# Two more seven-product steps in the first unit, one more in each of two branch units, and x's rows in two tiles

## The chip, the core and the metric

The kernel runs on one core of a Trainium2 chip. Its engines are named as the profile names them: PE (TensorE, matmuls), PEld (its weight loads), DVE (VectorE), ACT (ScalarE), POOL (GpSimd) and SP (SyncE, which here only issues transfers). The metric is the device time of one execution in microseconds (us).

## The reference

The reference is one hybrid decoder block on x of 256 tokens by 4096 channels, all in float32:

```
h    = rmsnorm(x) * norm_w
proj = h @ w_in                      # 4096 x 20480
u_p, z_p, u_c, b_c, c_c, z_c, g = split(proj)
y_pool = (pool(u_p) @ pool_w, by group) * pool_scale * silu(z_p)
y_conv = b_c * conv3(c_c * u_c) * silu(z_c)
br     = [y_pool @ w_branch[0], y_conv @ w_branch[1]]
merged = sum(sigmoid(g + gate_b) * br)
out    = rmsnorm(x + merged @ w_out) * final_norm_w
```

Nearly all of the work is three products with 256 rows on the left: by w_in, by the two w_branch and by w_out.

## The kernel before

**Units and steps.** The work is a list of units, each 1024 output columns wide: 20 of w_in (`cz0`, `cb0`, `cu0`, `cc0`, `cz1`, ... , the gates `g0_0` to `g1_0`), 8 of w_branch (`b0_0`, `b1_0`, `b0_1`, ... , `b1_3`) and 4 of w_out. A unit is a run of steps; each takes 256 input channels, and with them a 2 by 2 arrangement of weight blocks of 128 by 512. There are 16 steps in a unit of w_in or w_out and 8 in one of w_branch. A string of letters per unit says what kind each step is.

**Products in parts.** A float32 weight block is split in two: ACT writes the rounded "high" part to a cell of `ring` (the `highs` and `rounded` calls) and DVE writes the rest, the "low" part (`low`, `lows`: the profile's TENSOR_TENSOR ring<-raw,ring). The left operand was split in the same way earlier. One product is then three matmuls of 512 columns: high by high, high by low, low by high.

**P and S.** A plain step, P, has 4 blocks by 2 token halves, so 8 products or 24 matmuls, into four PSUM banks (`sums`). A step S does the same with seven products (Strassen's way, in Winograd's form), so 21 matmuls, into those banks and four more (`shared`). For an S step the weights have to be added up: POOL issues a transfer that adds one block to another as it lands (`gather` in `issue_corner`), DVE forms three sums in `parts`, ACT writes their high parts and DVE their low parts. At a unit's end ACT copies the four `shared` banks to tile `J` (`copy_corners`), DVE makes three sums there (`corner_sums`) and adds them to the unit's result (`combine`); a unit of P steps alone has none of that.

**The first unit.** `cz0` runs while x itself is still arriving. Its steps follow `FIRST`: operands 0 to 7 are kept as P operands, 8 to 15 as S operands, and in this unit all 16 are used as P. For an operand of the second kind ACT scales four blocks of x into `sa`, and DVE forms four sums there and writes high and low parts to `arena` (`x_fill`). Operands 14 and 15 have room for eight entries each; 8 to 13 have seven, and the eighth, needed by a P step, goes to a tile `extra`. Beside this, x's rows come in four quarters of 1 MB each into tile `E` (`fetch_rows`), and ACT and DVE square half of each (`square`) for the norm. `root` then gives `rin`, the factor of each token, and ACT scales by it as it empties the four banks into `Y` (`evacuate`; Y<-sums in the profile).

**The branch units.** The left operands of `b0_*` and `b1_*` come back from DRAM in pieces through small staging tiles (`sa`, `sb`, `sc`), as `Fill` objects that are advanced a little after every six matmuls (`pop_fill`). `b1_1` to `b1_3` run "PSPSPSPP", three S steps each. A P operand can also serve as S if its four sums lie in a tile `side`, as in the units of w_in with ten S steps.

**What sets the order.** Every instruction is pinned to the order in which the program makes it, on each engine. `pump` prepares weights up to four steps ahead, as far as the 26 cells of `ring` are free; `tick` pops one entry of a unit's epilogue queue after six matmuls. POOL's and SP's transfers leave in that order too, each behind whatever its engine waits for.

Of the kernel before, what the change touches and what calls it, by code (L numbers as in the profile page):

```python
# [15 lines left out]
P = 128  # L16
# [17 lines left out]
TAIL = 3  # L34

FIRST = (0, 1, 8, 2, 9, 3, 10, 11, 4, 12, 13, 5, 14, 6, 15, 7)
OPENED = 12
EIGHT3 = "PPPSPSSPSPSPSPSS"
NINE = "PSPSPSPSSPSPSSPS"
# [7 lines left out]
B0 = "PPPPSPSP"  # L47
B1 = "PSPSPSPP"
B1_FIRST = "PPSPSPSP"
B0_FOUR = "PPPSSPSS"  # L50


@with_exitstack
def hybrid_block(ctx: ExitStack, tc: tile.TileContext, x, xc, prm, rows_in, w_in, pool_w, w_branch, w_out, out):
# [17 lines left out]
    def sub(dst, a, b):  # L72
        return tt(dst, a, b, ALU.subtract)
# [10 lines left out]
    def move(dst, src):  # L84
        return pin(nc.scalar.dma_start(dst, src))
# [75 lines left out]
    def open_last(dt):  # L161
        stack = ExitStack()
        ctx.enter_context(stack)
        pool = stack.enter_context(tc.tile_pool(name="last", bufs=1, side="right"))
        last_pair.update(stack=stack, tile=pool.tile([P, 8 * KB], dt, name="last_pair"))
# [360 lines left out]
    def gap(n):  # L526
        return [None] * n
# [15 lines left out]
    def sequence(text, np_, total, both):  # L543
        text = [c for c in text if c in "PS"]
        ns = text.count("S")
        assert len(text) == total
        ss = list(range(np_, np_ + ns))
        ps = list(range(np_)) + list(range(np_ + ns, total))
        assert total - np_ - ns <= both
        return [(c, (ss if c == "S" else ps).pop(0)) for c in text]  # L550

    def seq_x(text):
        if text is FIRST:
            return [("P", i) for i in FIRST]
        if text is TEN_B:
            ss = list(range(ND, 13)) + [ND - 1] + list(range(13, 16)) + [ND - 2]
            ps = list(range(ND - 2))
            return [(c, (ss if c == "S" else ps).pop(0)) for c in "".join(text)]
        text = [c for c in text if c in "PS"]
        ns = text.count("S")  # L560
        if ns > NS + NB:
            ss = list(range(ND, 16)) + [resident[0]]
            if ns > NS + NB + 1:
                resident[0] = 2 * ND - 3 - resident[0]
                ss = [ss[-1]] + ss[:-1] + [resident[0]]
            ps = [i for i in range(ND) if i not in ss]
            return [(c, (ss if c == "S" else ps).pop(0)) for c in text]
        return sequence(text, ND, ND + NS + NB, NB)

    def seq_y(text):  # L570
        return sequence(text, 8 - text.count("S"), 8, 0)

    def in_unit(name, col, epi, text, **kw):
# [206 lines left out]
    def branch_unit(n, c):  # L780
        def epi(u):
            if n == 0:
                if c:
                    return gap(4) + [lambda: move(spare(), gates_d[1, c])] + gap(8) + [lambda: mul(Y, E, Y)]
                return gap(12) + [lambda: mul(Y, E, Y)]
            turned = spare() if c < 3 else Y

            def gated():
                mul(E, E, spare())
                if c == 3:  # L790
                    last_pair["stack"].close()
                    open_last(F32R)
                    last_pair["again"] = True

            def copy(j):
                act(chan(turned)[:, 2 * j:2 * j + 2], bankview(j))

            def stored():
                put(m_d[c], chan(turned))
                merged[c] = now[0] + (STORED if c == 3 else 2 * STORED)  # L800
            return gap(2) + [gated, None, lambda: add(E, E, Y), None,
                ] + gap(4) + pairs(transposes(E, copy)) + [
                    lambda: c < 3 and move(Y, gates_d[0, c + 1])] + gap(4) + [stored]

        text = (B1 if c else B1_FIRST) if n else (B0, B0_FOUR, B0_FOUR, B0_FOUR)[c]
        u = Unit(f"b{n}_{c}", lambda i: w_branch[n, c, i], seq_y(text), y_ops[n], epi)
        u.late = n == 0
        if not u.late:
            u.urgent, u.lead = (lambda: None), 3
        units.append(u)  # L810
# [30 lines left out]
    def copy(dst, src):  # L841
        return pin(nc.vector.tensor_copy(dst, src))
# [136 lines left out]
        stt(r, m, 1.5, r, ALU.add, ALU.mult)  # L979

    def fetch_rows(c):
        (aside if c else load)(E, xrows[:, :, c * NU:(c + 1) * NU])

    def square(c):
        q = E
        act(q[:, 0], q[:, 0], AF.Square, accum_out=ssq[:, 0, c:c + 1])
        stt(q[:, 1], q[:, 1], 1.0, q[:, 1], ALU.mult, ALU.mult, accum_out=ssq[:, 1, c:c + 1])

# [36 lines left out]
    def x_sums(j):  # L1025
        o = x_ops[first_order[j]]
        x_fill(o, sa)
        if o.n == 7:
            e = extra[:, o.region[1]]
            copy(e[:, 0], sa[:, A21])  # L1030
            sub(e[:, 1], sa[:, A21], e[:, 0].bitcast(F32))

    def item(fn, *args):
        return (None, None, lambda _: fn(*args))

    def before(i, fn, *args):
        steps[i].pre.append(item(fn, *args))

    for j in range(16):
        if j in staged:  # L1040
            steps[j - 1].mid += [item(x_scale, j), item(x_sums, j)]
        else:
            before(j, x_direct, j)
    for c in range(4):
        before(4 + 3 * c, fetch_rows, c)
        before(6 + 3 * c, square, c)

    def root():
# [142 lines left out]
    def run_step(u, st):  # L1191
# [8 lines left out]
        for i, g in enumerate(gs):  # L1200
# [2 lines left out]
                st.op.left -= 1  # L1203
            after_group(u, g[0], st, st is u.steps[-1] and st.kind == "P" and 3 <= i < len(gs) - 1)

    def open_side():
        stack = ExitStack()
        ctx.enter_context(stack)
        pool = stack.enter_context(tc.tile_pool(name="side", bufs=1))
        side.update(stack=stack, tile=pool.tile([P, 2, 4, P], F32R, name="side"))  # L1210

    for u in units:
        if u.name == "b0_0":
            last_pair["stack"].close()
            open_last(F32)
        if u is names["b1_3"]:
            lone.close()
            lone = ExitStack()
            ctx.enter_context(lone)
            pool = lone.enter_context(tc.tile_pool(name="lone", bufs=1))  # L1220
            fours.append(pool.tile([P, 4, P], F32, name="sd"))
            stages.append(pool.tile([P, 4, P], F32, name="se"))
        if u is names["o1"]:
            assert not fills
            lone.close()
            more.close()
            open_side()

            j, items = ND - 1, list(queue)
            queue.clear()  # L1230
            sides = (gap(HUSH) + [lambda: move(sa[:, 4:].rearrange("p o c -> p (o c)"),
                                                   m_d[j // 4][:, j % 4].rearrange("p k t -> p (k t)"))] + gap(8) + [
                lambda: sums_s(sa), None, None, lambda: act(side["tile"][:, 0], sa[:, 0:4]), None,
                lambda: sub(side["tile"][:, 1], sa[:, 0:4], side["tile"][:, 0].bitcast(F32))])
            items += gap(len(sides) - len(items))
            sides += gap(len(items) - len(sides))
            queue.extend([lambda a=a, b=b: (a and a(), b and b()) for a, b in zip(items, sides)])
        if u is names["g0_1"]:
            bands_open.close()
        if u is last_x:  # L1240
            side["stack"].close()
            more = ExitStack()
            ctx.enter_context(more)
            pool = more.enter_context(tc.tile_pool(name="more", bufs=1))
            stages.extend(pool.tile([P, 4, P], F32, name=name) for name in ("sb", "sc"))
            lone = ExitStack()
            ctx.enter_context(lone)
            apart["tile"] = lone.enter_context(tc.tile_pool(name="lone", bufs=1)).tile([P, 8 * P], F32R, name="apart")
            queue_fills()
        if u is last:  # L1250
            break
        for st in u.steps:
            assert st.prepared, (u.name, st.kind)
            if u is names["b0_3"] and st is u.steps[-1]:
                quiet[0] = now[0] + QUIET
            run_step(u, st)
            if u.text in (TEN, TEN_P) and st is next(q for q in u.main if q.kind == "S"):
                side_load(2 * ND - 3 - x_ops.index(st.op))
            state["now"] += 1
            if state["now"] == OPENED:  # L1260
                opening.close()
                open_side()
            pump()
            if u.before and st is u.steps[len(u.steps) * 3 // 4]:
                flush()
                u.before()
        flush()
        combine(u)
        queue.extend(u.epi(u))
        pump()  # L1270
# [114 lines left out]
```

## Time and profile before

| | before |
|---|---|
| median of 3 runs | 2341.66 us (2341.02 to 2343.1) |
| the profiled execution's own time | 2341.0 us |
| its span | 2339.3 us |
| PE busy | 2326.7 us (99%) |
| DVE busy | 2157.0 us (92%) |
| ACT busy | 1560.6 us (67%) |
| POOL busy | 309.2 us (13%) |
| granted clock | 0.999 |
| matmuls | 10372 |

The span runs from the first instruction of the program to the last; the time of an execution is some 2 us longer. A busy share near one says that an engine is hardly ever free, not that it is the one that others wait for: that is read from the chain of work that ended last and from what ended each engine's idle time.

### The profile page before, as it was taken

To read this page: it belongs to the slowest core of one execution; us is meant where nothing else is said; L and a number is where in the kernel's file an instruction comes from. 1 tells how busy PE (TensorE), PEld (TensorE's weight loads), DVE (VectorE), ACT (ScalarE), POOL (GpSimd) and SP (SyncE) were. 2 spreads that over 40 slices of the span, in tenths; PEclk is the share of its full clock that TensorE was granted. 3 is DMA by queue.
4 is the path that set the end of the run, shared out by engine and by line. 5 is a ranking of instruction groups with operands and counts; after the bars stand their busy time and mean duration, and the time that the engine had idled before them with its cause. 6 is when DMAs were issued, how large, how long until landed. Compare 5 with 4: busy or idle time off the path is not lost.

```text
span 2339.3 us, 29767 instructions
## 1 busy us (share of the span) xinstructions
PE 2326.7 (99%) x10372; PEld 1926.5 (82%) x10372; DVE 2157.0 (92%) x2117; ACT 1560.6 (67%) x1899; POOL 309.2 (13%) x369
## 2 busy tenths in 40 slices
PE   9999999999999999999999999999999999999998
PEld 7888888888888888888888888888888888888886
DVE  8899989999989979979999999998999889999998
ACT  6666766766666666666766767666776667676665
POOL 0111101221101211101121111111011010011110
PEclk9999999999999999999999999999999999999999
DMA  9889977989978968968999999999988889889998
GB/s 376 251 264 278 275 234 246 286 237 294 274 220 252 280 200 254 277 202 257 294 265 280 313 284 285 280 308 265 313 263 264 293 266 289 279 238 309 287 272 291
DMA packets 204983, 636.96 MB, mean 272 GB/s; under 512 B 21536, under 2 KB 29984, under 8 KB 202016
## 3 DMA queue, kind: packets, MB, share of 16 engines
q1 hardware_dynamic: 134912, 485.42, 59.0%
q0 software_dynamic: 52272, 107.76, 25.1%
q10 hardware_dynamic: 17648, 41.87, 4.8%
q8 instruction: 81, 1.33, 0.2%
q14 instruction: 70, 0.57, 0.1%
HBM read 587.78 MB, written 25.17 MB: 262 GB/s over the span
## 4 chain that ended last, share of the span: by engine, by line
PE 98%; DVE 1%; DMA 0%; ACT 0%; issue 0%; DVEq 0%; ACTq 0%; SPq 0%
PE sums L1140 68%; PE shared L1140 28%; PE shared L745 1%; PE shared L507 1%; DVE E L64 0%; DMA raw<-in_w_in_dram 0%; DMA Y<-in_xc_dram 0%; DVE ring L64 0%; DVE raw L1328 0%; PE shared L721 0%; ACT sa L61 0%; PE shared L722 0%; PE shared L724 0%; DVE J L64 0%; DVE J L1328 0%
## 5 line engine op out<-in xcount | busy, mean ns | idle before, releaser
L1140 PE MATMUL sums<-ring,arena 128*128 128x512 f32 x6663 | 1610.9, 390 | 1.1 <-DVE ring L64 0.7
L1140 PEld LDWEIGHTS sums<-ring,arena 128*128 128x128 f32 x6663 | 1248.2, 188 | 261.0 <-DVE ring L64 2.3
L64 DVE TENSOR_TENSOR ring<-raw,ring 128x1024 fp32r<-128x1024 f32 (+1 forms) x908 | 1088.2, 1215 | 70.9 <-ACT ring L61 61.7
L61 ACT ACTIVATE ring<-raw 128x1024 fp32r<-128x1024 f32 (+1 forms) x907 | 917.4, 1048 | 168.4 <-PE sums L1140 85.5
L61 ACT ACTIVATE ring<-parts 128x512 fp32r<-128x512 f32 (+1 forms) x501 | 406.4, 821 | 466.2 <-DVE parts L64 366.6
L1140 PE MATMUL shared<-ring,arena 128*128 128x512 f32 x2340 | 614.3, 389 | 0.0
L1140 PEld LDWEIGHTS shared<-ring,arena 128*128 128x128 f32 x2340 | 439.0, 188 | 91.3 <-DVE ring L64 0.2
L64 DVE TENSOR_TENSOR ring<-parts,ring 128x1536 fp32r<-128x1536 f32 (+2 forms) x273 | 426.0, 1569 | 38.0 <-ACT ring L61 27.2
L91 POOL DMA_DIRECT2D raw<-in_w_in_dram x182 | 158.7, 872 | 1356.5 <-DMA raw<-in_w_in_dram 729.7
L64 DVE TENSOR_TENSOR parts<-raw,parts 128x1024 f32<-128x1024 f32 x241 | 293.9, 1220 | 0.0
L64 DVE TENSOR_TENSOR parts<-raw 128x512 f32<-128x512 f32 x241 | 165.6, 687 | 5.2 <-DMA raw<-in_w_out_dram 2.5
L64 DVE TENSOR_TENSOR J<-J 128x512 f32<-128x512 f32 (+1 forms) x90 | 78.2, 869 | 31.7 <-ACT J L61 29.2
L1140 PE MATMUL shared<-ring,side 128*128 128x512 f32 x288 | 75.4, 389 | 0.0
L61 ACT ACTIVATE J<-shared 128x512 f32<-128x512 f32 x128 | 73.1, 605 | 2.9 <-PE shared L1140 1.0
L1140 PE MATMUL shared<-ring,last_pair 128*128 128x512 f32 x264 | 69.5, 389 | 0.0
L61 ACT ACTIVATE E<-sums 128x512 f32<-128x512 f32 x76 | 42.4, 599 | 35.7 <-PE sums L1140 32.6
L91 POOL DMA_DIRECT2D raw<-in_w_out_dram x33 | 29.5, 893 | 268.4 <-DVE ring L64 156.8
L1140 PEld LDWEIGHTS shared<-ring,side 128*128 128x128 f32 x288 | 54.1, 188 | 11.3
L1140 PE MATMUL sums<-ring,last_pair 128*128 128x512 f32 x246 | 63.0, 390 | 0.0
L91 POOL DMA_DIRECT2D raw<-in_w_branch_dram x26 | 22.5, 867 | 286.6 <-DMA raw<-in_w_branch_dram 150.7
L1140 PEld LDWEIGHTS shared<-ring,last_pair 128*128 128x128 f32 x264 | 49.5, 188 | 10.4
L1140 PEld LDWEIGHTS sums<-ring,last_pair 128*128 128x128 f32 x246 | 46.0, 188 | 10.0 <-DVE ring L64 0.5
(147 smaller groups left out, 748.5 us busy)
## 6 DMA issues: line engine op xcount, KB each, us to landing
raw<-in_w_in_dram SPq DMA_DIRECT2D x318, 768.0 KB, 6.8
raw<-in_w_in_dram SPq DMA_DIRECT2D x326, 256.0 KB, 5.7
raw<-in_w_branch_dram SPq DMA_DIRECT2D x64, 768.0 KB, 7.0
raw<-in_w_out_dram SPq DMA_DIRECT2D x64, 768.0 KB, 8.0
raw<-in_w_in_dram POOLq DMA_DIRECT2D x182, 256.0 KB, 7.1
raw<-in_w_branch_dram SPq DMA_DIRECT2D x64, 256.0 KB, 5.5
raw<-in_w_out_dram SPq DMA_DIRECT2D x64, 256.0 KB, 6.9
E<-J POOLq DMA_DIRECT2D x30, 512.0 KB, 12.6
```

What stands on the lines that cost most here:

```text
L61: return pin(nc.scalar.activation(dst, src, func, **kw))
L64: return pin(nc.vector.tensor_tensor(out=dst, in0=a, in1=b, op=op))
L91: return pin(nc.gpsimd.dma_start(dst, src, accum_op=ALU.add))
L507: pin(nc.tensor.transpose(shared(j)[:, i * T + t * P:i * T + (t + 1) * P], src[:, t, c:c + P], ident))
L745: pin(nc.tensor.matmul(o, a, b, start=(k, i) == (0, 0), stop=(k, i) == (3, 2)))
L1140: pin(nc.tensor.matmul(ps, lhs, rhs, start=n == 0, stop=n == u.total[b] - 1))
```

## The change

Four things are changed.

1. In the first unit, operands 14 and 15 (its 13th and 15th step) are used as S. That unit now also has `shared` banks to copy, to sum and to add.
2. x's rows: the second and the fourth quarter go to `J`, the first and the third stay in `E`. The fourth quarter is asked for in the preparation of step 11, where it was step 13.
3. The eighth entry of operands 8 to 13 (`extra`) is written after the low parts of the step's weights, no longer before.
4. `b1_1` and `b1_2` run "PSPSSPSP", four S steps each. The fourth uses operand 4, a P operand, with its sums in `side`. That tile is opened from `b0_1` to `b0_3` in the place of the staging tiles `sb` and `sc`, which are opened again after.

The diff:

```diff
+FIRST_S = (14, 15)
...
+B1_FOUR = "PSPSSPSP"
...
         if text is FIRST:
-            return [("P", i) for i in FIRST]
+            return [("S" if i in FIRST_S else "P", i) for i in FIRST]
...
     def seq_y(text):
+        if text is B1_FOUR:
+            ss, ps = [5, 6, 7, 4], list(range(4))
+            return [(c, (ss if c == "S" else ps).pop(0)) for c in text]
         return sequence(text, 8 - text.count("S"), 8, 0)
...
-        text = (B1 if c else B1_FIRST) if n else (B0, B0_FOUR, B0_FOUR, B0_FOUR)[c]
+        text = (B1_FIRST, B1_FOUR, B1_FOUR, B1)[c] if n else (B0, B0_FOUR, B0_FOUR, B0_FOUR)[c]
...
     def fetch_rows(c):
-        (aside if c else load)(E, xrows[:, :, c * NU:(c + 1) * NU])
+        (aside if c else load)(rows_at(c), xrows[:, :, c * NU:(c + 1) * NU])
+
+    def rows_at(c):
+        return J.rearrange("p (t n) c -> p t (n c)", t=2) if c % 2 else E
 
     def square(c):
-        q = E
+        q = rows_at(c)
...
     def x_sums(j):
         o = x_ops[first_order[j]]
         x_fill(o, sa)
-        if o.n == 7:
-            e = extra[:, o.region[1]]
-            copy(e[:, 0], sa[:, A21])
-            sub(e[:, 1], sa[:, A21], e[:, 0].bitcast(F32))
+
+    def x_extra(j):
+        o = x_ops[first_order[j]]
+        e = extra[:, o.region[1]]
+        copy(e[:, 0], sa[:, A21])
+        sub(e[:, 1], sa[:, A21], e[:, 0].bitcast(F32))
...
             steps[j - 1].mid += [item(x_scale, j), item(x_sums, j)]
+            if x_ops[first_order[j]].n == 7:
+                steps[j].mid.append(item(x_extra, j))
...
     for c in range(4):
-        before(4 + 3 * c, fetch_rows, c)
+        before(4 + 3 * c - (2 if c == 3 else 0), fetch_rows, c)
         before(6 + 3 * c, square, c)
...
+        if u is names["b0_1"]:
+            assert all(f.at is None for f in fills)
+            more.close()
+            del stages[1:]
+            open_side()
+            items = list(queue)
+            queue.clear()
+            sides = gap(4) + [lambda: move(sa[:, 4:].rearrange("p o c -> p (o c)"),
+                                           y_d[1, 1][:, 0].rearrange("p k t -> p (k t)"))] + gap(9) + [
+                lambda: sums_s(sa)] + gap(3) + [lambda: act(side["tile"][:, 0], sa[:, 0:4]), None,
+                lambda: sub(side["tile"][:, 1], sa[:, 0:4], side["tile"][:, 0].bitcast(F32))]
...
+        if u is names["b0_3"]:
+            side["stack"].close()
+            open_more()
```

What it does to the order is seen at three places. The first is POOL's queue at the program's start. Its first transfers before, with the semaphores that each waits for (DMAHW and DMASW count landings, DVE and Activation the finished work of DVE and ACT):

```order
masks.py:199 AFFINE_SELECT ident<-ident 128x128 [waits Pool_49]
L88 DMA E<-in_x_dram 128x2x1024 [waits DMAHW4_49,DVE_49,Activation_49]
L88 DMA E<-in_x_dram 128x2x1024 [waits DMASW0_49,DVE_49,Activation_49]
L91 DMA raw<-in_w_in_dram 128x512 [waits DMAHW0_49,DVE_49]
L88 DMA E<-in_x_dram 128x2x1024 [waits DMASW1_49]
L91 DMA raw<-in_w_in_dram 128x512 [waits DMAHW4_49,DVE_49]
```

And now:

```order
masks.py:199 AFFINE_SELECT ident<-ident 128x128 [waits Pool_49]
L90 DMA J<-in_x_dram 128x2x1024
L93 DMA raw<-in_w_in_dram 128x512 [waits DMAHW4_49,DVE_49]
L90 DMA E<-in_x_dram 128x2x1024
L90 DMA J<-in_x_dram 128x2x1024 [waits DMASW0_49,DVE_49,Activation_49]
L93 DMA raw<-in_w_in_dram 128x512 [waits DMAHW2_49,DVE_49]
```

The second quarter's transfer, which waited until `E` had been squared, goes to a tile that nothing has used, and waits for nothing. The third and the fourth now stand between the transfers of the two S steps.

The second place is DVE in the first unit where two operands of the S kind follow each other (here operands 10 and 11; the rows begin with the end of operand 10's preparation). Before:

```order
L842 CAST arena<-sa 128x896
L64 TENSOR_TENSOR arena<-sa,arena 128x896
L842 CAST extra<-sa 128x128
L64 TENSOR_TENSOR extra<-sa,extra 128x128
L76 SCALAR_TENSOR_TENSOR E,ssq<-E 128x1024
L64 TENSOR_TENSOR ring<-raw,ring 128x1024 x2
L64 TENSOR_TENSOR sa<-sa 128x128 x4
L842 CAST arena<-sa 128x896
```

And now:

```order
L847 CAST arena<-sa 128x896
L66 TENSOR_TENSOR arena<-sa,arena 128x896
L78 SCALAR_TENSOR_TENSOR E,ssq<-E 128x1024
L66 TENSOR_TENSOR ring<-raw,ring 128x1024 x2
L847 CAST extra<-sa 128x128
L66 TENSOR_TENSOR extra<-sa,extra 128x128
L66 TENSOR_TENSOR sa<-sa 128x128 x4
L847 CAST arena<-sa 128x896
```

The last reads of `sa` for operand 10 (the two rows on `extra`) now stand right ahead of the sums for operand 11, which are formed in the same `sa` after ACT has written it.

The third place is ACT at the end of the first unit. Before, from the norm's square root to the first emptied bank:

```order
L61 ACT_TABLE_LOAD
L61 ACTIVATE rin_s<-rin_m 128x2
L61 ACTIVATE ring<-raw 128x1024 x4
L61 ACTIVATE Y<-sums_83,rin 128x512
L61 ACTIVATE Y<-sums_85,rin 128x512
```

And now:

```order
L63 ACT_TABLE_LOAD
L63 ACTIVATE rin_s<-rin_m 128x2
L63 ACTIVATE ring<-raw 128x1024
L63 ACTIVATE J<-shared_87 128x512
L63 ACTIVATE ring<-raw 128x1024
L63 ACTIVATE J<-shared_86 128x512
L63 ACTIVATE ring<-raw 128x1024
L63 ACTIVATE J<-shared_89 128x512
L63 ACTIVATE J<-shared_88 128x512
L63 ACTIVATE ring<-raw 128x1024
L63 ACTIVATE Y<-sums_83,rin 128x512
L63 ACTIVATE Y<-sums_85,rin 128x512
```

Four copies of the `shared` banks stand between the square root and the emptying of the `sums` banks, all of them behind the square root.

More of the change, by code (lines that the diff above doesn't have):

```diff
@@ L1204, in run_step, with open_more @@
             after_group(u, g[0], st, st is u.steps[-1] and st.kind == "P" and 3 <= i < len(gs) - 1)
+    def open_more():
+        nonlocal more
+        more = ExitStack()
+        ctx.enter_context(more)
+        pool = more.enter_context(tc.tile_pool(name="more", bufs=1))
+        stages.extend(pool.tile([P, 4, P], F32, name=name) for name in ("sb", "sc"))
+    more = None
     def open_side():
@@ L1215, in hybrid_block @@
             open_last(F32)
+        if u is names["b0_1"]:
[9 more added lines that the diff above has]
+                lambda: sub(side["tile"][:, 1], sa[:, 0:4], side["tile"][:, 0].bitcast(F32))]
+            items += gap(len(sides) - len(items))
+            sides += gap(len(items) - len(sides))
+            queue.extend([lambda a=a, b=b: (a and a(), b and b()) for a, b in zip(items, sides)])
+        if u is names["b0_3"]:
+            side["stack"].close()
+            open_more()
         if u is names["b1_3"]:
+            assert all(f.at is None for f in fills)
+            more.close()
             lone.close()
-            lone = ExitStack()
-            ctx.enter_context(lone)
-            pool = lone.enter_context(tc.tile_pool(name="lone", bufs=1))
+            del stages[1:]
+            open_more()
+            pool = more.enter_context(tc.tile_pool(name="lone", bufs=1))
             fours.append(pool.tile([P, 4, P], F32, name="sd"))
@@ L1224, in hybrid_block @@
             assert not fills
-            lone.close()
             more.close()
@@ L1241, in hybrid_block @@
             side["stack"].close()
[L1242 to L1245, printed above, removed]
             lone = ExitStack()
@@ L1248, in hybrid_block @@
             apart["tile"] = lone.enter_context(tc.tile_pool(name="lone", bufs=1)).tile([P, 8 * P], F32R, name="apart")
+            open_more()
             queue_fills()
```

## The prediction

> **What bounds the kernel now.** I read the page's busy shares and groups first, then the chain of work that ended last, then the waits of PE.
>
> ```profile
> span 2339.3 us, 29767 instructions
> PE 2326.7 (99%) x10372; PEld 1926.5 (82%) x10372; DVE 2157.0 (92%) x2117; ACT 1560.6 (67%) x1899; POOL 309.2 (13%) x369
> ...
> 18.11 81.67 PE sums L1140 x359
> 104.55 5.44 PE sums L1140 x24
> ...
> PE sums L1140 <- DVE ring L64: 0.7, 1, 0.7
> PE sums L1140 <- DVE ring L842: 0.5, 1, 0.5
> ```
>
> From 18.11 us on the chain is PE alone, and PE waits 1.1 us in all behind its first product, both times near the start. So time is won only by fewer matmuls, 5.44 / 24 = 0.227 us each, and lost wherever PE is made to wait. DVE, 92% busy, is the engine that could make it wait. For the stretches that the change touches I read the busy times by window:
>
> ```profile
> 0.00:20.00 20.00, 17.76 (x80) 13.71 (x81) 13.71 (x27) 12.83 (x21) 0.70 (x6) 1.00 0.90 316
> 20.00:60.00 40.00, 40.00 (x179) 33.10 (x178) 39.31 (x68) 28.07 (x43) 1.61 (x2) 1.00 1.01 402
> 1740.00:1830.00 90.00, 90.00 (x407) 74.67 (x406) 83.16 (x73) 59.10 (x75) 9.40 (x10) 1.00 0.91 282
> 1910.00:2000.00 90.00, 90.00 (x407) 74.67 (x406) 83.28 (x85) 58.28 (x78) 8.54 (x9) 1.00 0.89 280
> ```
>
> After the window come its length, the busy time of PE, PEld, DVE, ACT and POOL, the clock, the share of the DMA engines and GB/s. In the first 60 us the DMA engines are full, and from 20 to 60 us DVE has 0.7 us free in 40. In the two windows over the changed branch units it has 6.8 and 6.7 us free in 90.
>
> **The change part by part.** *Matmuls.* Four steps go from 24 to 21: 12 x 0.227 = -2.7 us, half of it in the first unit (-1.36), half in `b1_1` and `b1_2`.
>
> *The second quarter at the start.* Where loads set the pace at the start:
>
> ```profile
> 1.09 0.29 POOL masks.py:199 TENSOR_SCALAR_AFFINE_SELECT ident<-ident 128x128 f32<-128x128 f32 x1
> 35.76 0.87 POOL L88 DMA_DIRECT2D E<-in_x_dram  x1 [34.38 <-ACT sa L61]
> ...
> 15.42 2.01 ACT L61 ACTIVATE ring<-raw 128x1024 fp32r<-128x1024 f32 x2 [1.80 <-DMA raw<-in_w_in_dram]
> ...
> 16.38 0.22 DVE L842 CAST extra<-sa 128x128 fp32r<-128x128 f32 x1
> 16.63 0.29 DVE L64 TENSOR_TENSOR extra<-sa,extra 128x128 fp32r<-128x128 f32 x1
> 16.84 2.35 DVE L64 TENSOR_TENSOR ring<-raw,ring 128x1024 fp32r<-128x1024 f32 x2
> ...
> 18.11 3.48 PE L1140 MATMUL sums<-ring,arena 128*128 128x512 f32 x14 [0.65 <-DVE ring L64]
> ...
> L61 ACT ACTIVATE ring<-raw 128x1024 fp32r<-128x1024 f32 (+1 forms) x907 | 917.4, 1048 | 168.4 <-PE sums L1140 85.5
> ```
>
> POOL sent this quarter at 35.76, after 34.38 us of waiting; now it waits for nothing and leaves when POOL has made `ident`, at about 1.4 us. The third step's weights are what ACT waits for at 15.42, then DVE's low part, then PE at 18.11. The quarter is 128 x 2048 x 4 bytes = 1.05 MB, ahead of those weights. If the DMA engines share their rate, it costs between 1.05 / 402 = 2.6 us (the full window) and 1.05 / 316 = 3.3 us (the first window, start-up included; at its share of 0.90 taken as full, 351 GB/s and 3.0 us); if its bytes fit beside the others, 0. I take 2.8, between 2.6 and 3.0, as a share of 0.90 leaves no room for bytes beside the others. The moved `extra` rows give a little back: the low part can start when ACT's first half is done (15.42 + 1.05) and not at 16.84, 0.37 sooner. PE's third step comes 2.8 - 0.37 = 2.4 us later, and DVE, which still does the same rows, 2.9 later. [...]
>
> *`extra` behind the low parts.* DVE's rows are the same ones, but where two S operands follow each other (10 and 11, 12 and 13) the sums in `sa` must wait for ACT, and ACT for the last read of `sa`:
>
> ```profile
> 35.02 2.36 DVE L64 TENSOR_TENSOR ring<-raw,ring 128x1024 fp32r<-128x1024 f32 x2
> 37.29 1.02 DVE L64 TENSOR_TENSOR sa<-sa 128x128 f32<-128x128 f32 x4
> ...
> 35.24 0.89 ACT L61 ACTIVATE sa<-Y,par 128x256 f32<-128x256 f32 x2
> ```
>
> Today ACT's 0.89 us lies under DVE's low parts. Now DVE stands still for it, with a hand-over on both sides: I take 1.05 us, twice, so 2.1 us (at least 0 if DVE has waited anyway, at most 2 x 1.3). This is from 35 to 55 us, where DVE has nothing free, so from then on it is 2.9 + 2.1 = 5.0 us late, PE only 2.4.
>
> *Two S steps in DVE's queue.* Its rows from there on:
>
> ```profile
> 63.85 1.22 DVE L76 SCALAR_TENSOR_TENSOR E<-E 128x1024 f32<-128x1024 f32 x1
> 64.99 2.36 DVE L64 TENSOR_TENSOR ring<-raw,ring 128x1024 fp32r<-128x1024 f32 x2
> 67.27 0.88 DVE L76 SCALAR_TENSOR_TENSOR arena<-Y,par,arena 128x256 fp32r<-128x256 f32 x2
> 68.06 2.36 DVE L64 TENSOR_TENSOR ring<-raw,ring 128x1024 fp32r<-128x1024 f32 x2
> 70.33 1.02 DVE L64 TENSOR_TENSOR sa<-sa 128x128 f32<-128x128 f32 x4
> 73.25 2.35 DVE L64 TENSOR_TENSOR ring<-raw,ring 128x1024 fp32r<-128x1024 f32 x2
> 82.59 1.22 DVE L76 SCALAR_TENSOR_TENSOR E<-E 128x1024 f32<-128x1024 f32 x1 [6.19 <-DMA E<-in_x_dram]
> 84.78 2.36 DVE L64 TENSOR_TENSOR ring<-raw,ring 128x1024 fp32r<-128x1024 f32 x2 [0.96 <-ACT ring L61]
> 87.06 0.15 DVE L973 TENSOR_REDUCE rin_m<-ssq 128x2 f32<-128x8 f32 x1
> 90.92 0.68 DVE L64 TENSOR_TENSOR parts<-raw 128x512 f32<-128x512 f32 x1
> 96.58 1.76 DVE L64 TENSOR_TENSOR ring<-parts,ring 128x1536 fp32r<-128x1536 f32 x1 [1.57 <-ACT ring L61]
> 98.25 2.35 DVE L64 TENSOR_TENSOR ring<-raw,ring 128x1024 fp32r<-128x1024 f32 x2
> ```
>
> An S step costs DVE 0.60 + 3 x 1.14 + 1.67 = 5.7 us (starts from 90.92 on: 0.60 for the first sum, 1.14 for each piece of 1024, 1.67 from 96.58 to 98.25), a P step 2.27. The 6.2 us that DVE waited for the fourth quarter are gone, as that is asked for sooner. Walked on from 63.85 + 5.0 = 68.85: square 1.14, S step 5.7 and a hand-over of 0.1, operand 13's low 0.79, P step 2.27, operand 15 for 2.92 (70.33 to 73.25), S step 5.75, the last operand 0.79, square 1.15. That is 89.5, where the last step's low parts start (84.78 before). The first is there at 90.7. PE reaches the last step at 88.75 - 1.36 + 2.4 = 89.8 and needs it one matmul later: a stall of 0.65 us.
>
> *Behind the square root.* The unit's end before:
>
> ```profile
> 87.45 0.20 ACT L61 ACTIVATE rin_s<-rin_m 128x2 f32<-128x2 f32 x1 [0.45 <-DVE rin_m L974]
> 87.56 3.89 ACT L61 ACTIVATE ring<-raw 128x1024 fp32r<-128x1024 f32 x4
> 92.39 2.68 ACT L61 ACTIVATE Y<-sums,rin 128x512 f32<-128x512 f32 x4 [0.94 <-ACT ring L61]
> 88.75 11.04 PE L1140 MATMUL sums<-ring,arena 128*128 128x512 f32 x48
> L61 ACT ACTIVATE J<-shared 128x512 f32<-128x512 f32 x128 | 73.1, 605 | 2.9 <-PE shared L1140 1.0
> ```
>
> The next unit's first matmul, 24 after 88.75, is at 94.19; the bank it writes was emptied by 93.0, so 1.2 us early. Now DVE ends the last low parts at 91.7, the norm's sum follows, and ACT's root 0.39 us later (87.06 to 87.45) at 92.1. Behind it stand the four roundings (3.88) and four copies of 0.52 (605 ns less 0.09 us, by which ACT's instructions overlap: 3.89 us for four of 1048 ns), and only then the first bank: 92.24 + 3.88 + 2.07 = 98.2, empty at 98.8. PE would be ready at 89.8 + 0.65 + 5.44 = 95.9 and waits 2.9 us. Two scalings by `rin` and three sums (5 us of DVE) come after; DVE's own sums are needed only at the next S step's second half, some 8 us on, so I cost them at nothing; without that cover they'd cost up to 2 us.
>
> *`b1_1` and `b1_2`.* Each new S step adds 3.4 us of DVE, one to each window, and the 6.7 us free there cover it; the side tile adds 1.01 us (four sums in `sa`, as at 70.33) and a subtraction once. I take the full gain, -1.36; if DVE's free time lies at the wrong places, each unit loses up to 2 us.
>
> *Sum.* The next unit starts at 98.85 and not 94.19: +4.66, in which the first unit's saving is contained. With -1.36 that is +3.3 us on the profiled execution's 2341.0 (span 2339.3), so 2344.3. The median of the runs is 0.66 above it: **2345.0 us**.
>
> **The rivals.** *The early quarter costs twice its bytes.* It goes in rows of 4 KB against the weights' 2 KB pieces at the start, and could take more than its share just when the first blocks are due, then leave ACT with work heaped up: 5.5 us late instead of 2.8, all of it passed to DVE, hence to the square root, 2347.7. It decides, so that the time is over 0.2% longer, from about 4.2 us of delay on. For it: DMA at 0.90 to 1.01. Against: bytes delay bytes only once.
>
> *The quarter is free.* The sum loses 2.9: 2342.1. For it: the first window moves 86 GB/s less than the second. Against: ACT waits 1.80 us for a load there.
>
> *Everything is hidden.* If neither the quarter nor ACT's copies cost anything, only the matmuls and 0.37 count: -3.1, 2338.6. For it: ACT is busy 67%. Against: the copies stand behind the root in ACT's order. This is also the most that can be gained, so a gain of over 0.2% (4.7 us, about what a measurement of this kernel can tell from no change) has no mechanism.
>
> *The branch units turn to DVE's pace.* Each adds 2 us rather than saving 0.68: +5.4 on the forecast's end, 2350.4. For it: DVE is at 92%, and these units add to it. Against: 6.7 us free in 90.
>
> **How the numbers follow.** The forecast's mechanism gets 0.62, of which 0.05 lies above 2346.3 (its own hand-overs slower than taken); the early quarter at double cost 0.12; the free quarter 0.14; everything hidden 0.05; the branch units 0.05; gains that I can't name 0.02. Slower by over 0.2%: 0.05 + 0.12 + 0.05 = 0.22. Faster: 0.02. Within: 0.76. The range 2341.2 to 2347.2 takes in the free quarter and the near part of the slower cases.
>
> **What would show it.** In the changed profile: POOL's transfer to `J` before 3 us; the third step's wait on PE some 2 us longer; DVE gaps of 1 us ahead of two groups of sa<-sa, ended by ACT; a DVE row of rin_m near 91.7; and a PE wait of about 3 us ended by ACT's Y<-sums, near 96 us. From there a chain of PE alone. If PE has no wait near 96 us, the forecast is wrong and the time is below 2342; waits between 1740 and 2000 us would speak for the last rival.

## The result, and the profile after

The changed kernel takes **2346.55 us** (median of 12 runs, 2345.06 to 2350.31) beside 2341.47 us for the kernel before (12 runs, 2340.69 to 2343.28): ratio **1.0023, 95% interval 1.0015 to 1.0031**, so 5.1 us longer. The forecast was 2345.0, with 2341.2 to 2347.2 as its range; it had +3.3 us on the profiled execution where the medians differ by +5.1. The profiled execution of the changed kernel took 2348.27 us, which is 1.7 us above its own median; that is kept apart below.

The page of the changed kernel, the busy times:

```profile
PE 2327.9 (99%) x10360; PEld 1924.8 (82%) x10360; DVE 2176.6 (93%) x2145; ACT 1564.9 (67%) x1914; POOL 311.5 (13%) x373
```

PE executes 12 matmuls fewer (10360, 10372 before) and yet is busy 1.2 us longer. Twelve times 0.227 us should have taken 2.7 us away: a first sign that some matmuls became slower.

PE's waits of the changed kernel (us in total, times, longest):

```profile
PE sums L1152 <- ACT Y L63: 2.4, 1, 2.4
PE sums L1152 <- DVE ring L66: 1.6, 3, 1.1
PE sums L1152 <- DVE ring L847: 1.5, 1, 1.5
...
```

The third row is the start; the second holds the last step (1.09), 0.21 at the start and 0.25 at 168 us. The first row is the wait behind the square root that the prediction described. Where it stands is read from PE's timeline, first of the changed kernel, then of the kernel before (start, us from first start to last end, the group, and in brackets the idle time ahead of it and what ended it):

```profile
20.28 3.47 PE L1152 MATMUL sums<-ring,arena 128*128 128x512 f32 x14 [0.21 <-DVE ring L66]
...
91.04 5.55 PE L1152 MATMUL sums<-ring,arena 128*128 128x512 f32 x23 [1.09 <-DVE ring L66]
99.00 7.32 PE L1152 MATMUL sums<-ring,arena 128*128 128x512 f32 x24 [2.40 <-ACT Y L63]
106.15 0.84 PE L1152 MATMUL shared<-ring,arena 128*128 128x512 f32 x3
```

```profile
88.75 11.04 PE L1140 MATMUL sums<-ring,arena 128*128 128x512 f32 x48
99.63 0.84 PE L1140 MATMUL shared<-ring,arena 128*128 128x512 f32 x3
```

Before, the 48 matmuls of the two units run through, and the second 24 start at 88.75 + 5.44 = 94.19. Now they start at 99.00 (**+4.81**) and the next group does not follow 5.44 us later but 7.15 (99.00 to 106.15): another **+1.71 us** in which PE waits for nothing. What it is, the windows of one microsecond of the changed kernel show; after the window come its length, busy time and instructions of PE, PEld, DVE, ACT and POOL, the granted clock, the DMA engines' share and GB/s:

```profile
99.00:100.00 1.00, 1.00 (x4) 0.87 (x5) 1.00 (x2) 1.00 (x3) 0.00 (x0) 0.94 0.87 320
100.00:101.00 1.00, 1.00 (x4) 0.71 (x4) 1.00 (x2) 1.00 (x3) 0.00 (x0) 0.50 0.87 320
...
102.00:103.00 1.00, 1.00 (x4) 0.81 (x3) 1.00 (x2) 0.32 (x1) 0.00 (x0) 0.50 0.74 154
103.00:104.00 1.00, 1.00 (x5) 0.79 (x5) 0.95 (x2) 1.00 (x2) 0.00 (x0) 0.85 0.52 152
```

From 99.9 to 103.3 us the clock that PE is granted is half: 2 x (0.06 + 3 x 0.50 + 0.15) = 3.4 us at 0.50, which costs 3.4 x 0.5 = 1.7 us. In the kernel before the clock is 1.00 throughout this stretch; its window there:

```profile
99.00:103.00 4.00, 4.00 (x19) 3.33 (x18) 3.41 (x5) 3.99 (x5) 0.86 (x1) 1.00 0.73 206
```

This term stood in no part of the prediction.

The steps ahead of it are as foretold. The unit's end on ACT in the changed kernel:

```profile
92.43 0.20 ACT L63 ACTIVATE rin_s<-rin_m 128x2 f32<-128x2 f32 x1 [1.15 <-DVE rin_m L979]
...
93.49 0.57 ACT L63 ACTIVATE J<-shared 128x512 f32<-128x512 f32 x1
...
98.24 2.44 ACT L63 ACTIVATE Y<-sums,rin 128x512 f32<-128x512 f32 x4
```

The root at 92.43 (predicted 92.1), four roundings and four copies behind it, the first bank of Y at 98.24 (predicted 98.2), PE at 99.00 (predicted 98.85).

From there on (106.15 against 99.63, an offset of 6.52 us) the two traces differ by a nearly constant amount, apart from the branch units and 1.5 us, most of which is found below. PE at the same groups ahead of `b1_1` and behind `b1_2`, before and after:

```profile
1660.51 2.20 PE L1140 MATMUL sums<-ring,last_pair 128*128 128x512 f32 x9
...
1989.65 10.59 PE L1140 MATMUL sums<-ring,arena 128*128 128x512 f32 x46
```

```profile
1668.54 2.20 PE L1152 MATMUL sums<-ring,last_pair 128*128 128x512 f32 x9
...
1996.32 4.01 PE L1152 MATMUL sums<-ring,arena 128*128 128x512 f32 x17
```

The offset is 8.03 us ahead of them and 6.67 behind: 1.36 us won, all that 6 x 0.227 can give.

The sum for the medians' difference is then 4.81 + 1.71 - 1.36 = **5.16**, against 5.08 measured; as the terms come from one execution and the executions spread over 5 us, an agreement to 0.1 us is in part chance. The profiled execution lost more, above all 1.19 us between 166 and 172 us (21 matmuls, from 165.99 to 171.94, took 5.95 us instead of 4.76). Its chain of waits there (start, us, what), and then ACT and PE:

```profile
154.66 10.41 DMA side_d<-side
```

```profile
165.09 0.63 ACT L63 ACTIVATE side<-sa 128x512 fp32r<-128x512 f32 x1 [5.01 <-DMA side_d<-side]
...
169.99 0.73 PE L1152 MATMUL shared<-ring,last_pair 128*128 128x512 f32 x2 [0.34 <-DVE ring L66]
```

The write of `side` to DRAM took 10.41 us; ACT must not overwrite `side` until it has landed, DVE stands behind ACT, and PE behind DVE. In the twelve runs below ACT's wait at this place is 0 to 3.1 us, and PE waits in one of them, 0.33 us. It is a reason for this one execution to lie above the median.

### The profile page after: what moved, and what is told of

It is laid out like the page before. It is cut to its first block, busy times and chain, and to the rows that moved or that the text cites. A ratio compares the mean times of both kernels' runs of the same rounds, so it can differ in the third digit from the quotient of the medians.

```text
span 2346.6 us, 29824 instructions
## 1 busy us (share of the span) xinstructions
PE 2327.9 (99%) x10360; PEld 1924.8 (82%) x10360; DVE 2176.6 (93%) x2145; ACT 1564.9 (67%) x1914; POOL 311.5 (13%) x373
## 4 chain that ended last, share of the span: by engine, by line
PE 92%; DVE 3%; DMA 3%; ACT 1%; issue 1%; ACTq 0%; SPq 0%; DVEq 0%; POOL 0%; POOLq 0%
PE sums L1152 63%; PE shared L1152 27%; DMA raw<-in_w_in_dram 2%; DVE ring L66 1%; PE shared L750 1%; DMA Y<-in_xc_dram 1%; ACT ring L63 1%; PE shared L509 1%; DVE parts L66 1%; DMA side_d<-side 0%; DVE E L66 0%; DVE sa L66 0%; DVE raw L1364 0%; PE shared L726 0%; ACT sa L63 0%
## 5 line engine op out<-in xcount | busy, mean ns | idle before, releaser
L63 ACT ACTIVATE ring<-parts 128x1024 fp32r<-128x1024 f32 (+1 forms) x511 | 413.7, 820 | 490.4 <-DVE parts L66 403.5
L66 DVE TENSOR_TENSOR ring<-parts,ring 128x1536 fp32r<-128x1536 f32 (+2 forms) x283 | 433.1, 1541 | 34.1 <-ACT ring L63 23.4
L66 DVE TENSOR_TENSOR parts<-raw,parts 128x1024 f32<-128x1024 f32 x245 | 298.6, 1219 | 0.0
L1152 PE MATMUL shared<-ring,side 128*128 128x512 f32 x306 | 80.1, 389 | 0.0
```

The source lines that it names most:

```text
L63: return pin(nc.scalar.activation(dst, src, func, **kw))
L66: return pin(nc.vector.tensor_tensor(out=dst, in0=a, in1=b, op=op))
L1152: pin(nc.tensor.matmul(ps, lhs, rhs, start=n == 0, stop=n == u.total[b] - 1))
```

## Experiments

The theory: the early quarter delays PE and DVE, the `extra` rows and the S steps delay DVE alone; so the root is late, the four copies behind it make it later, PE stands still for 2.4 us, and because it stands still its clock is halved for the 3.4 us after. The rivals are named with each run. Each time below is the median of 11 runs (6 for the longest wait), beside runs of the kernel before on the same chip; a + or - is the difference to their median.

### The parts taken back one at a time

**The second quarter when E is free.**

```diff
-        return J.rearrange("p (t n) c -> p t (n c)", t=2) if c % 2 else E
+        return J.rearrange("p (t n) c -> p t (n c)", t=2) if c == 3 else E
```

> The changed kernel, but the second quarter of x's rows goes into E again, so it leaves when E is free (35.76 us in the profile before) and not at 1.56 us; the third and fourth stay as changed. Theory (the early quarter delays the third step's weights and this reaches the end of the first unit): PE's third step at about 18.1 us instead of 20.28, DVE some 2.5 us earlier from then on, the root and the next unit's first matmul some 2.2 to 2.5 us earlier (about 96.6 instead of 99.00), the wait behind the root as long as it is (2.4 us): 2346.5 - 2.3 = 2344.2. Rival (the delay is absorbed before the root, the loss is all made at the unit's end): the next unit still starts at 99, 2346.5.

Measured 2344.02 us, +3.1 on the kernel before (ratio 1.0012, 1.0003 to 1.0021). PE's timeline of this run:

```profile
17.69 3.47 PE L1152 MATMUL sums<-ring,arena 128*128 128x512 f32 x14 [0.43 <-DVE ring L66]
...
96.23 7.32 PE L1152 MATMUL sums<-ring,arena 128*128 128x512 f32 x24 [2.45 <-ACT Y L63]
103.39 0.84 PE L1152 MATMUL shared<-ring,arena 128*128 128x512 f32 x3
```

The third step is back at 17.69, the next unit starts 2.77 us earlier than in the changed kernel, and everything at its end is unchanged: the wait of 2.45, and the 24 matmuls in 7.16 us, the clock at 0.50 for 3.4 us of them. So the delay of the start goes through to the unit's end in full, and neither the wait nor the low clock needs it.

**`extra` ahead of the low parts.**

```diff
         x_fill(o, sa)
+        if o.n == 7:
+            x_extra(j)
...
-            if x_ops[first_order[j]].n == 7:
-                steps[j].mid.append(item(x_extra, j))
```

> The changed kernel, but the extra rows stand ahead of the low parts again. Theory (DVE's two gaps of 1.02 and 1.03 us ahead of sa<-sa are paid in full at the root, as DVE sets it): both gaps gone, the root 2 us earlier (90.4 instead of 92.43), PE's wait at the last step 0 instead of 1.09 us, the next unit's first matmul at about 97.0 instead of 99.00, its wait 0.7 to 1.0 instead of 2.40. If the low clock after that wait (24 matmuls in 7.15 us rather than 5.44) comes from the wait's length, it is gone too: 2346.5 - 2.0 - 1.7 = 2342.8; if it does not hang on the wait, 2344.5. Rival (the gaps only take time in which DVE would have waited anyway): no change, 2346.5.

Measured 2342.95 us, +2.1 (1.0011, 1.0002 to 1.0020). DVE's timeline of the changed kernel has the two gaps that this is about:

```profile
41.38 1.02 DVE L66 TENSOR_TENSOR sa<-sa 128x128 f32<-128x128 f32 x4 [1.02 <-ACT sa L63]
...
57.68 1.02 DVE L66 TENSOR_TENSOR sa<-sa 128x128 f32<-128x128 f32 x4 [1.03 <-ACT sa L63]
```

In this run the same two groups begin at 39.62 and 54.74 with no wait. Its PE:

```profile
89.71 5.60 PE L1152 MATMUL sums<-ring,arena 128*128 128x512 f32 x24
96.05 5.74 PE L1152 MATMUL sums<-ring,arena 128*128 128x512 f32 x24 [0.73 <-ACT Y L63]
101.62 0.84 PE L1152 MATMUL shared<-ring,arena 128*128 128x512 f32 x3
```

The stall at the last step is gone, the wait is 0.73 us, and the 24 matmuls behind it take 5.57. From 57.68 to 54.74 DVE is 2.94 us earlier; 0.30 of that is an earlier start of this execution (15.98 against 16.28 at the first sums in `sa`), so the order of these rows is worth 2.6 us, the upper bound of the prediction (2 x 1.3) and not its 2.1.

The times fall into two groups, six of 2342.2 to 2343.0 and five of 2344.6 to 2346.8; the profiled one (2345.71) is of the second, and its trace says why. From the chain of waits:

```profile
767.07 16.81 DMA Y<-J
```

One accumulating transfer of POOL took 16.81 us, ACT stood 4.17 us for it, and PE 1.78 us in three waits; against the kernel before PE is 2.7 us later behind them (796.28 and 791.54) than ahead (773.85 and 771.82). That the other executions of the longer group lost theirs here too is not shown.

**No S steps in the first unit.**

```diff
-FIRST_S = (14, 15)
+FIRST_S = ()
```

> The changed kernel without the two S steps in the first unit (16 P steps as before, so 6 matmuls more there); the early quarter, the extra rows behind the low parts and the branch units stay as changed. Theory (the S steps lengthen DVE's queue and put four copies behind the root; the clock falls after the wait that this makes): no J copies behind the root, no wait there, no low clock; PE carries only the start's +2.2 us, so the next unit's first matmul at 94.19 + 2.2 = 96.4 and the time 2341.5 + 2.2 - 1.4 = 2342.3. Rival (the low clock and the 1.2 us lost near 166 us come with the delayed start, not with the S steps): 2345.

Measured 2342.02 us, +1.1 (1.0006, 0.9997 to 1.0014). PE's timeline:

```profile
90.47 11.04 PE L1152 MATMUL sums<-ring,arena 128*128 128x512 f32 x48
101.35 0.84 PE L1152 MATMUL shared<-ring,arena 128*128 128x512 f32 x3
```

The 48 matmuls run through again, at a clock of 1.00. What is left is the late start: 90.47 - 88.75 = 1.72 us, less the 1.36 of the branch units, so +0.4, which the interval does not tell from the +1.1 measured. So the stall, the wait and the low clock need the S steps; the rival, by which they come with the late start, falls.

**The branch units alone.** The kernel before with `b1_1` and `b1_2` as changed (the three edits above taken back, and the quarters as before).

```diff
-        text = (B1 if c else B1_FIRST) if n else (B0, B0_FOUR, B0_FOUR, B0_FOUR)[c]
+        text = (B1_FIRST, B1_FOUR, B1_FOUR, B1)[c] if n else (B0, B0_FOUR, B0_FOUR, B0_FOUR)[c]
```

> The kernel before with nothing but the branch units' part: b1_1 and b1_2 with four S steps each and the side tile; the first unit as before. Theory (PE sets the pace there, DVE has the room): 6 matmuls of 0.227 us fewer, -1.36: 2341.5 - 1.4 = 2340.1, PE's offset against the kernel before 0 up to 1750 us and -1.36 behind 2000. Rival (these units turn to DVE's pace): up to +2 us each, 2345.

Measured 2340.32 us, -0.6 (0.9997, 0.9988 to 1.0006): the interval holds both -1.4 and no change, so the median decides nothing. The trace does:

```profile
1660.41 2.20 PE L1152 MATMUL sums<-ring,last_pair 128*128 128x512 f32 x9
...
1988.19 12.18 PE L1152 MATMUL sums<-ring,arena 128*128 128x512 f32 x53
```

The offset to the kernel before goes from -0.10 to -1.46: 1.36 us, in full. The rival (DVE's pace) would have shown a wait of PE here; there is none.

### The wait and the clock

**The copies into J behind Y's banks.**

```diff
-        if u.s and u is not last:
+        if u.s and u is not last and u is not units[0]:
             corner_sums(u)
```

> The changed kernel, but ACT copies the four banks of the first unit into J after it has emptied the four banks of Y, and not ahead. Theory (the four copies of 0.5 us behind the root make PE's wait of 2.40 us, and the wait makes the low clock): Y<-sums starts 2.1 us earlier (96.2 instead of 98.24), PE's wait is 0.3 us or a little more, the 24 matmuls behind it take about 5.5 us instead of 7.15: 2346.5 - 2.1 - 1.7 = 2342.7. Rival one (the low clock has nothing to do with the wait): 2344.4. Rival two (DVE, whose three sums in J now wait for later copies, is late with the next steps' low parts and PE waits there instead): 2345 to 2346.5.

Measured 2344.31 us, +3.0 (1.0014, 1.0005 to 1.0023). In the profiled execution Y<-sums starts at 95.92 (98.24; 0.41 us of the difference are an earlier root, at 92.02), PE waits 0.46 us, and the 24 matmuls take 5.59 (96.64 to 102.23): 3.9 us earlier than in the changed kernel at the same group. The copies make the wait, as the theory has it. The median came 1.6 us above the theory's 2342.7. In the profiled execution 1.2 us go near 120 us, where PE waits twice for DVE's low parts (0.64 us by the waits, 1.2 by PE's rows: 102.23 to 123.16 is 20.93 us, and 99.63 to 119.35, the same matmuls of the kernel before, 19.72). That is rival two, in a small size; the rest is not assigned.

**PE kept busy through the wait.** Ten matmuls, whose result is never read, between the last step and the wait.

```diff
+KEEP = 10
...
+        if u is units[0]:
+            o = x_ops[first_order[15]]
+            for n in range(KEEP):
+                pin(nc.tensor.matmul(shared(1), o.standing(0, 0)[0], o.view[:, 0, 0:4], start=True, stop=True))
         flush()
         combine(u)
```

> The changed kernel with ten more matmuls (0.227 us each, their result is never read) on PE between the last step of the first unit and the wait for Y, into a bank that has been copied by then: PE works through most of the 2.4 us in which it stood. Theory (the granted clock falls because PE stands still, and the next matmuls run at it): the wait is under 0.3 us, the 24 matmuls behind it take 5.44 to 5.7 us instead of 7.15 and begin at the same 99.0; the granted clock from 99 to 103 us is 1.00 and not 0.61: 2346.5 - 1.6 = 2344.9. Rival (the matmuls there are slow for another reason, such as ACT reading the banks or the DMA traffic of that stretch): still 7.15 us, 2346.5 or 0.2 more.

Measured 2344.46 us, +3.1 (1.0013, 1.0004 to 1.0022), 2.0 less than the changed kernel by each one's own kernel before. PE's timeline and the windows of this run:

```profile
96.41 2.43 PE L1307 MATMUL shared<-arena 128*128 128x512 f32 x10
98.98 5.73 PE L1153 MATMUL sums<-ring,arena 128*128 128x512 f32 x24
104.55 0.84 PE L1153 MATMUL shared<-ring,arena 128*128 128x512 f32 x3
```

```profile
99.00:103.00 4.00, 4.00 (x18) 3.31 (x19) 4.00 (x5) 2.51 (x5) 0.00 (x0) 1.00 0.90 274
```

The 24 matmuls begin at 98.98, as before the edit at 99.00, with ACT, DVE and the DMA engines doing the same (0.90 of their time, 0.88 in the changed kernel from 99 to 103). They take 5.57 us instead of 7.15, at a clock of 1.00 instead of 0.61. Nothing but PE's standing still was taken away, so **the low clock comes from that**, and ten useless matmuls are worth 1.6 us here.

**The wait put into the kernel before.** Copies on ACT ahead of the first Y<-sums and nothing else: three, seven or ten.

```diff
     def evacuate(u, t, n):
+        if u is units[0] and not u.flags.get("held"):
+            u.flags["held"] = True
+            for _ in range(7):
+                act(J[:, 0], E[:, 0, 0:NH])
```

> As the run with seven copies, with three: 2 us of ACT's time behind the root, which by that run (4.6 us of copies made a wait of 1.64) fits into the 3 us that the bank is empty ahead of PE's need. Theory (only PE's standing still costs): no wait, PE's rows at the times of the kernel before, 2341.3. Rival (ACT's copies cost by delaying ACT): 2342 to 2343.

> The kernel before with nothing but seven copies of 0.52 us on ACT (of rows that lie in E, into the unused J) behind the root's roundings and ahead of the first Y<-sums: the bank is empty 3.6 us later, 96.6 instead of 93.0, and PE, ready at 94.19, waits 2.4 us. Theory (such a wait is paid twice, as time and as the clock that is lower behind it): PE's wait 2.4 us, the granted clock behind it about 0.6 for some 4 us, PE 2.4 + 1.7 = 4.1 us late from then on: 2341.0 + 4.1 = 2345.1. Rival (a wait costs its length): 2343.4.

> As the run with seven copies, with ten: 2 us more of ACT, so a wait of 3.6 us instead of 1.64. Theory (from some 2 us of wait on the clock falls: 2.40 and 2.45 us had it, 0.46, 0.73 and 1.64 had not): the granted clock behind it about 0.6 for 4 us, the 24 matmuls 7.1 us or more instead of 5.57, the time 2341.3 + 3.6 + 1.7 = 2346.6. Rival (the clock does not hang on the length of the wait): 5.57 us, 2344.9.

The times are 2341.77 (ratio 1.0000, 0.9991 to 1.0009), 2345.07 (1.0014, 1.0005 to 1.0022) and 2348.19 us (1.0030, 1.0018 to 1.0042). With three copies PE has no wait at this place. PE with seven, and with ten copies, and the windows with ten:

```profile
95.77 5.73 PE L1144 MATMUL sums<-ring,arena 128*128 128x512 f32 x24 [1.64 <-ACT Y L61]
101.34 0.84 PE L1144 MATMUL shared<-ring,arena 128*128 128x512 f32 x3
```

```profile
98.28 7.36 PE L1144 MATMUL sums<-ring,arena 128*128 128x512 f32 x24 [4.22 <-ACT Y L61]
105.48 0.84 PE L1144 MATMUL shared<-ring,arena 128*128 128x512 f32 x3
```

```profile
98.00:99.00 1.00, 0.71 (x2) 0.62 (x3) 0.00 (x0) 1.00 (x3) 0.00 (x0) 0.72 1.12 330
99.00:100.00 1.00, 1.00 (x3) 0.76 (x3) 0.00 (x0) 1.00 (x3) 0.29 (x1) 0.50 0.89 369
...
101.00:102.00 1.00, 1.00 (x4) 0.80 (x3) 0.54 (x1) 1.00 (x2) 0.00 (x0) 0.58 0.52 102
```

A wait of 4.22 us costs 4.22 and then again 7.20 - 5.44 = 1.76: the clock is at 0.50 for 2 x (0.28 + 0.50 + 0.50 + 0.42) = 3.4 us, the same stretch as after 2.40 and 2.45 us. In these three traces the price is the same, not proportional to the wait. At the end of this execution PE stands 6.57 us behind the kernel before (5.85 at 105.48), near the median's +6.9. Of the 1.6 us by which the theory's 3.6 + 1.7 falls short, 0.6 are the longer wait and 0.7 come after 105.48.

With seven copies the wait was 1.64 us and not the 2.4 that I had worked out (the root came at 86.63 in this execution, 87.45 in the one that I had used), and in the profiled execution, 2342.81 us, the matmuls behind it take 5.57 at a clock of 1.00: a wait alone. That execution is the fastest of eleven, though; the others lie from 2344.1 to 2347.7, so the expected 2345.1 was met by the median while the profile shows none of the mechanism. That in those the clock fell is likely by the size, and not shown.

**From how long a wait on.** In the profiled executions the clock stayed at 1.00 behind waits of 0.46, 0.73 and 1.64 us, and was 0.50 for 3.4 us behind waits of 2.40, 2.45 and 4.22 us, each seen once. No trace shows a wait of this kind between 1.64 and 2.40 us, and none shows that the length alone decides: behind PE's last matmul of the changed kernel, which ends at 2335.91, the clock is still 1.00 for 3.1 us and 0.50 from 2339.0 on, although 2.40 us of standing still near 97 were followed by half clock.

### Putting it right

**Repaired.** The three edits above together: the second quarter when E is free, `extra` ahead of the low parts, the copies behind Y's banks; the S steps of the first unit and of the branch units stay. **The first unit alone** is the same with three S steps in `b1_1` and `b1_2`, as before (the sums for the side tile are still formed, though not used there):

```diff
-        text = (B1_FIRST, B1_FOUR, B1_FOUR, B1)[c] if n else (B0, B0_FOUR, B0_FOUR, B0_FOUR)[c]
+        text = (B1_FIRST, B1, B1, B1)[c] if n else (B0, B0_FOUR, B0_FOUR, B0_FOUR)[c]
```

> The changed kernel with the second quarter sent when E is free, the extra rows ahead of the low parts, and the copies into J behind Y's: the two S steps of the first unit and the branch units stay. Theory (these three are all that the change lost): the root at about 87.6, Y's first bank empty at about 92.2, PE there at 94.19 - 1.36 = 92.8 without a wait, no low clock; both savings of 1.36 us kept: 2341.0 - 2.7 = 2338.3, 0.9988 of before. Rival (with six S-step rows more in DVE's queue the low parts of the next unit's first steps come late): PE waits 1 to 2 us between 90 and 110, about 2340.

> The repaired kernel with the branch units of before (three S steps in b1_1 and b1_2): of the change only the two S steps of the first unit and x's last quarter in the second tile are left. Theory (each saving of six matmuls is worth 1.36 us where nothing waits): 2341.3 - 1.4 = 2339.9, the next unit's first matmul at 94.19 - 1.4 = 92.8. Rival (the first unit's saving is lost again where DVE works off its longer queue, between 100 and 125 us): 2341.3.

Repaired: **2339.83 us, ratio 0.9990, 0.9981 to 0.9999**: 1.5 us faster than the kernel before, and the only version here whose interval lies below 1. The first unit alone: 2340.43 us (0.9995, 0.9986 to 1.0004), -0.9 where -1.4 was expected; its second 24 matmuls start at 92.4 (86.96 + 5.44), without a wait, and the interval does not tell -1.4 from nothing. PE and ACT of the repaired kernel, and PE at the groups ahead of `b1_1` and behind `b1_2`:

```profile
87.25 11.04 PE L1152 MATMUL sums<-ring,arena 128*128 128x512 f32 x48
98.13 0.84 PE L1152 MATMUL shared<-ring,arena 128*128 128x512 f32 x3
```

```profile
87.18 0.20 ACT L63 ACTIVATE rin_s<-rin_m 128x2 f32<-128x2 f32 x1 [1.16 <-DVE rin_m L979]
```

```profile
1660.77 2.20 PE L1152 MATMUL sums<-ring,last_pair 128*128 128x512 f32 x9
...
1988.55 15.80 PE L1152 MATMUL sums<-ring,arena 128*128 128x512 f32 x69
```

The root stands at 87.18 (87.45 before, 92.43 as changed), there is no wait and no low clock, and the next unit's second step is 99.63 - 98.13 = 1.50 us earlier. So both savings are there: 1.50 at this place, and 1.36 over the branch units (from 1660.77 - 1660.51 = +0.26 to 1988.55 - 1989.65 = -1.10). But between 98 and 1660 us this execution loses 1.76 us, more than the first saving. 0.60 of that go from 114 to 119 us, where PE waits 0.16 us for DVE's low parts (from 98.13 to 118.45 is 20.32 us, and from 99.63 to 119.35, before, 19.72). The same place costs 0.59 in the first unit alone and 1.21 with the copies behind (near 120 us), and nothing in the kernels that copy ahead of Y. So it goes with the later copies: DVE's three sums in `J` then start 5.2 us behind the next unit's first matmul (97.60 against 92.4 in the first unit alone) and not 2.0 us ahead of it (96.97 against 99.00 in the changed kernel). Another 0.93 go near 1460 us, with a wait of PE of 0.63, and the rest in smaller pieces. The expected 2338.3 was 1.5 us too low.

**The early quarter alone**, in the kernel before (the sums for the side tile are formed here too, and not used in the branch units):

```diff
+        return J.rearrange("p (t n) c -> p t (n c)", t=2) if c == 1 else E
```

> The kernel before with nothing but the second quarter of x's rows in the second tile, so that it leaves at 1.6 us. Theory (1.05 MB ahead of the first weights cost 2.2 us at PE's third step, and there is no wait in which PE could win them back): third step at 20.3 instead of 18.11, the next units 2.2 us later, no wait near 95, 2341.3 + 2.2 = 2343.5. Rival (what is lost at the start is won back because the later quarters are there sooner): 2341.3 to 2342.

Measured 2343.81 us, +2.5 (1.0011, 1.0002 to 1.0020). PE's timeline:

```profile
20.66 3.47 PE L1152 MATMUL sums<-ring,arena 128*128 128x512 f32 x14 [0.63 <-DVE ring L66]
...
91.28 11.04 PE L1152 MATMUL sums<-ring,arena 128*128 128x512 f32 x48
```

The third step is 2.55 us late (18.11 before), and 91.28 - 88.75 = 2.53 us are still there at the end of the unit: as much as the median is longer (2.5). The later quarters win nothing back.

## Why the prediction was right, and where it was not

- **What bounds the kernel before.** Right, with one loose reading: of the 1.1 us that PE waits "behind its first product", 0.46 stand ahead of it, at 6.04. Nothing hangs on it.
- **The quarter leaves at once and delays the third step** (2.4 us for PE, from 2.8 us of bytes). Right: it left at 1.56 us, and the third step came 2.17 us later in the changed kernel's profile, 2.55 alone; DVE was 2.63 us late (24.81 against 22.18 at the sums in `sa`) and not 2.9. The delay starts earlier than I had it, at the first block (PE's first product at 6.87, 6.04 before). The rivals "free" and "twice its bytes" both fall.
- **The `extra` rows cost DVE 2 x 1.05 us.** Right in place and mechanism (gaps of 1.02 and 1.03, ended by ACT); with what lies around them 2.6 instead of 2.1. The two errors nearly cancel: at the square of x's third quarter DVE was 69.12 - 63.85 = 5.27 us late, 5.0 by the prediction.
- **The stall at the last step, 0.65 us.** It was 1.09: the last low parts started at 89.77 instead of 89.5, and PE was there 0.2 us sooner.
- **The root, the copies behind it, a wait of 2.9 us, the next unit at 98.85.** Right in mechanism: 2.40 and 99.00. The +4.66 measured +4.81. That the first bank came at 98.24 for 98.2 is partly luck: the root was 0.3 us later than predicted, and the roundings and copies behind it took 5.70 us instead of 5.95.
- **DVE's scalings and three sums behind the root, at nothing.** Right for this kernel: PE waits for nothing from 106.15 to 166 us. The cover is thin, though: with the copies moved behind Y, PE loses 0.6 to 1.2 us near 115 to 121.
- **The branch units' -1.36.** Right, -1.36 in the three traces shown; the rival "DVE's pace" falls.
- **What failed: "the sum".** The prediction ended PE's loss where PE's wait ended, and said of the time after it "From there a chain of PE alone". The chain is PE alone, but at half clock for 3.4 us: 1.71 us that no term held. 4.81 + 1.71 - 1.36 = 5.16, against 5.08 measured; without the missing term the sum would have been 3.45, near the 3.3 forecast. It moved the result from inside the 0.2% to just over it (the interval, 1.0015 to 1.0031, reaches to both sides), for which the prediction had given 0.05 + 0.12 + 0.05, none of it for this cause. That the time still lies in the range, 0.65 us below its end, is luck: the end of 2347.2 was drawn for other cases.

Open is how often, over the executions, a wait of 1.64 us or more makes the clock fall, and whether the losses of the repaired kernel's profiled execution are those of its median (1.5 us won and not 2.7).

## What to carry to other kernels

In this kernel, which PE bounds, a wait of PE had two prices: its length, and behind the waits of 2.40, 2.45 and 4.22 us also 1.71 to 1.76 us of half clock; in another kernel that PE bounds, both are worth a look in the trace. A wait that could not be removed was better filled with matmuls that nobody reads (2.0 us here). On an engine whose work is pinned to the program's order (here ACT), what must follow a late value (the banks that PE waits for, behind the root) goes ahead of what merely could run then, such as the copies into J: Y's first bank began 3.90 us behind the root with the copies behind it, and 5.81 with the copies ahead. And a load that is asked for sooner "because its buffer is free" was paid for where the DMA engines were full (a share of 0.90 over the first 20 us of the kernel before): 1.05 MB cost 2.5 us to the end here.

## What the runs showed of the hardware

- PE's granted clock was 0.50 for 3.4 us after it stood still 2.40, 2.45 or 4.22 us, and 1.00 after 0.46, 0.73 and 1.64 us (one execution each). The half clock began 0.9, 0.0 and 0.2 us after PE's first matmul behind the wait, and cost 1.71 to 1.76 us.
- With ten matmuls in the place of the 2.40 us, the clock was 1.00 from 99 to 103 us and not 0.61. Behind PE's last matmul of the changed kernel (2335.91) it was 0.50 from 2339.0 on, 3.1 us later.
- Of POOL's transfers of 0.5 MB, the write of `side` took 10.41 us (DMA share 0.88 over them) in the changed kernel's trace, and an accumulation into Y 16.81 in the trace with `extra` ahead of the low parts; the median of the twelve accumulations into Y is 12.0 in the trace of the kernel before and 11.7 in the changed kernel's. ACT waited 5.01 and 4.17 us for the two, and PE, over DVE, lost 1.2 and 2.7 us there. In the twelve runs below the changed kernel ACT's wait for `side` is 0 to 3.1 us, and PE waits there in one, 0.33 us.
